# Two-layer decoder trunk on one core: first weight chunk plain, ScalarE's order unforced, one convolution tap on ScalarE, output projection all in high and low parts

## The chip, the cores and the metric

The kernel runs on one core of one Trainium2 chip. A core has a matrix engine (TensorE, PE), a vector engine (VectorE, DVE), a scalar engine (ScalarE, ACT), a general engine (GpSimd, POOL) and a queue engine (SyncE, SP) that issues the transfers from main memory. Each engine works through its own list of instructions in order and waits on semaphores for the others. The metric is the device time of one execution in microseconds; lower is better.

## What is computed

One sequence of 256 tokens with 1024 features goes through two layers. Each layer is a half-step SwiGLU feed-forward block, a token mixer, and another half-step feed-forward block. The mixer of layer 0 is stick-breaking attention, that of layer 1 a recurrent block (RG-LRU). Each block's input is normed and then scaled and shifted by numbers that come from a conditioning vector through a large matrix (`mod_w`), and its output is gated likewise. Everything is float32.

```python
for layer in range(DEPTH):
    mod = (c_act @ mod_w[layer] + mod_b[layer]).reshape(B, N_SUB, 3, D_MODEL)
    h, g = sublayer_input(x, norm_g[layer, 0], mod[:, 0])
    x = x + MACARON_W * g * swiglu(h, ffn_w_gu[layer, 0], ffn_w_down[layer, 0])
    h, g = sublayer_input(x, norm_g[layer, 1], mod[:, 1])
    y = mixer(h)
    x = x + g * y
    h, g = sublayer_input(x, norm_g[layer, 2], mod[:, 2])
    x = x + MACARON_W * g * swiglu(h, ffn_w_gu[layer, 1], ffn_w_down[layer, 1])
return rmsnorm(x, final_norm_g)
```

The recurrent block, cut to what the change touches (`xp` is `xb` with three zeros ahead of the first token, so that `conv_w[3]` is the tap on a token's own value):

```python
gate, xb = jnp.split(h @ w_in, 2, axis=-1)
xc = conv_b + xp[:, 0:S] * conv_w[0]
for tap in range(1, CONV_W):
    xc = xc + xp[:, tap:tap + S] * conv_w[tap]
r, i = sigmoid(blockwise xc @ w_r + b_r), sigmoid(blockwise xc @ w_i + b_i)
a = exp(-LRU_C * r * softplus(-lam)); b = sqrt(1 - a * a) * (i * xc)
hs = scan(a, b)
y = (gelu(gate) * hs) @ w_out
```

## The kernel before

Features lie on the 128 partitions and tokens along the free side, so x is eight tiles of 128 x 256. A weight block of 128 x 2048 (1 MB) is fetched by one transfer into one of three `raw` buffers.

**High and low parts.** Most products are made from parts. `load` (L510) converts each 1024-column half of a raw block into a high part `wh` on ACT (L525, a copy into a shorter format) and a low part `wl = raw - wh` on DVE (L528). Seven buffers of each kind stand in a ring. Activations are split alike, hi on ACT and lo on DVE. `Acc.group` (L541) then issues three matmuls for each product: wh with hi, wh with lo, wl with hi. `group32` (L565) instead issues one plain float32 matmul from unsplit data; the trace shows two instructions for it.

**The planner.** The program is not written in the order in which it runs. `Program.op` records each operation with an engine, a modelled cost, what it reads and writes and, with `after`, operations that it must follow. `schedule` (L170) then runs a model of the engines and emits the operations in the order of their modelled starts. An operation of ACT or DVE gets its due time from the PE work that needs it. So a change of one operation or of one ring can move others.

**Start.** `first_loads` (L1240) fetches the conditioning vector and x. Four small matmuls on zeros (`warm(EARLY)`), then two products that spread the vector over the partitions (L1247), then the sum of squares for the norm (`rstd`, L624 to L630) and eighteen more small matmuls (`warm(LATE)`, L842) run on PE. `norm_chunk` (L651) makes the first normed chunk: hp on DVE (L656), hi on ACT, lo on DVE (L658). The first feed-forward block starts by going through its first eight output tiles (SQ = 8) one input chunk k at a time, as the chunks arrive (L837 to L865): 16 groups for each k, into eight accumulators. The 1 MB of weights for chunk k come interleaved with the two 0.5 MB tiles of `mod_w` that chunk k + 1 needs. `early` (L800) reduces such a tile on DVE (L585) and makes a scale or a shift on ACT (`mf`). `first_chunk` (L822) makes hi and hp from them on ACT (seen as `hx<-arenaf,mf,mf` and `hpre<-arenaf,mf,mf`) and lo on DVE (L832). Chunks 0 and 7 (`SMALL`) come in four pieces of 512 columns, the others in two halves. For k = 1, 2, 3 (`FREE`) and the `SMALL` ones the order of ACT is left to the planner; for k = 4, 5, 6 both ACT operations of `first_chunk` must follow the conversion of the chunk's second half (`splits[:1]`, L858). After the first group of chunks 1, 3, 5, 7 `kick_op` (L740) issues one tiny matmul, which marks the chunk's beginning in the trace.

**Mod tiles.** The other 128 tiles of `mod_w` (0.5 MB each) are fetched all along the first two thirds of the kernel into a ring `rawm` of four buffers, and each is reduced by one DVE operation (L585) and one short one that reads its accumulator. They share SP's queue and DVE with the weights. The ring also holds the gate weights of the recurrent block (three loads) and, at the start, the conditioning vector.

**Recurrent block.** `rglru` (L1081) projects xb in five tiles; `conv` (L1089) has ACT write xb into one of two buffers and DVE make the four taps (L1095 for the first with the bias, L1098 for the others). `gates` (L1102) makes two plain products and three ACT functions for each of ten blocks, and a product on DVE (L1127) that frees one of the three buffers in which i stands. `decay`, `scan` and `output` (L1165 to L1197) are ordered by ACT's function tables: all exponentials, then all square roots, then all Gelu. Meanwhile PE makes four gate projections. `output(0)` ends with the DVE product L1189, which gives y0, the first of five blocks of 256 features. With `N32 = 1` block 0 and its weights stay unsplit, and `down` (L672) takes them with `group32`; the blocks after it are split (L1194, L1195) and go through `group`. `down` runs the first three blocks one after the other and the last two by pairs of output tiles, and then adds the result to x (L695).

Of the kernel before, what the change touches and what calls it, by code (L numbers as in the profile page):

```python
# [34 lines left out]
SMALL = (0, 7)  # L35
EARLY, LATE = 4, 18
KICK0, FREE = (1, 3, 5, 7), (1, 2, 3)
HXPAD, HKPAD, ARPAD = 112, 16, 56
# [331 lines left out]
def trunk(ctx, tc, xT, cb, par, modw, gu0, gu, wdn, qk, wv, wo, win, wri, wout, out):  # L370
# [22 lines left out]
    rawr, _ = ring("raw", 3, CH)  # L393
    modr, _ = ring("rawm", 4, D)
    whr, _ = ring("wh", 7, HALF, F32R)
# [111 lines left out]

    splits = []

    def load(src, n, name, chain=None, size=HALF):  # L510

        raw = Buf(rawr, name=f"raw_{name}")
        part = None
        if chain is None:
            dma(lambda: raw()[:, :n], src, n, [raw])
        res = []
        for a in range(0, n, size):
            m = min(n - a, size)
            if chain is not None:
                part = a  # L520
                chain(lambda a=a, m=m: raw()[:, a : a + m], src[:, a : a + m], m, [(raw, a)])
            h, lo = Buf(whr, name=f"wh_{name}"), Buf(wlr, name=f"wl_{name}")

            def fh(h=h, a=a, m=m):
                act.activation(h()[:, :m], raw()[:, a : a + m], AF.Copy)  # L525

            def fl(h=h, lo=lo, a=a, m=m):
                dve.tensor_tensor(lo()[:, :m], raw()[:, a : a + m], f32(h()[:, :m]), ALU.subtract)  # L528

            splits[:] = [pr.op("ACT", c_act(m), fh, [(raw, part)], [h]), V(fl, m, [(raw, part), h], [lo])]  # L530
            res.append((h, lo))
        return res
# [117 lines left out]

    def norm_chunk(gen, d, q):  # L651
        gs, sh = mfin[gen + (1,)], mfin[gen + (0,)]
        hp, hi, lo = Buf(hpr), Buf(hxr), Buf(hxr)
        hcur.setdefault(gen, []).append((hi, lo))
        c = slice(d, d + 1)
        V(lambda: dve.scalar_tensor_tensor(hp(), x[d](), gs()[:, c], q(), ALU.mult, ALU.mult), T, [x[d], (gs, d), q], [hp], ptr=1)  # L656
        A(lambda: hi()[:, :T], hp, AF.Identity, T, [hp, (sh, d)], [hi], ptr=1, bias=lambda: sh()[:, c])
        V(lambda: dve.scalar_tensor_tensor(lo()[:, :T], hp(), sh()[:, c], f32(hi()[:, :T]), ALU.add, ALU.subtract), T,  # L658
          [hp, (sh, d), hi], [lo], ptr=1)

    def norm(gen, q):
# [118 lines left out]
    def ffn(l, s, nxt, hook):  # L780
# [11 lines left out]
        if j == 0:  # L792
# [7 lines left out]
            def early(k, w):  # L800
# [20 lines left out]

            def first_chunk(k, after=()):  # L822

# [8 lines left out]
                pr.op("DVE", c_dve(T), lambda: dve.tensor_tensor(lo()[:, :T], hp(), f32(hi()[:, :T]), ALU.subtract), [hp, hi],  # L832
                      [lo])

            early(0, 1)
            early(0, 0)
            for k in range(KD):  # L837
                if k == 4:
                    chained(lambda: pars()[:, NP0:], par[:, NP0:], NPAR - NP0, [(pars, 1)])
                if k == 0:  # L840
                    norm_chunk((0, 0), k, q)
                    warm(LATE, [pr.last_pe])  # L842
                    for ks in xq_parts:
                        normed(ks)
                elif k in SMALL:
                    first_chunk(k)
# [234 lines left out]
    def rglru(l, s, nxt):  # L1081
        N32 = 1
        R, F = new_phase(8 * (NB - N32), 86)
# [5 lines left out]
        def conv(n, evict):  # L1089
            xb = Buf(xbr)  # L1090
            evict(n % 2, xb)
            if n % 2 == 0:
                xc[n // 2] = Buf(F, 4)
            c, e, cs = of(xc, n)
            V(lambda: dve.tensor_scalar(c()[:, cs], xb()[:, 1 : 1 + T], col(OFF_CW + n), col(OFF_CB + n), ALU.mult,  # L1095
                                        ALU.add), T, [xb, pars], [(c, e)], ptr=2)
            for tap in range(1, 4):
                V(lambda tap=tap: dve.scalar_tensor_tensor(c()[:, cs], xb()[:, 1 + tap : 1 + tap + T],  # L1098
# [141 lines left out]
    def first_loads(F):  # L1240
# [4 lines left out]
        for h in range(2):  # L1245
            cs = slice(h * 512, (h + 1) * 512)
            pr.op("PE", 1870.0, lambda h=h, cs=cs: pe.matmul(b[h]()[:, :], ones[:1, :], c()[:1, cs], start=True, stop=True),  # L1247
                  [c], [b[h]])
# [117 lines left out]
```

## Time and profile before

| | us |
|---|---|
| median of 3 runs | 962.55 |
| lowest and highest of the runs | 962.23, 963.67 |
| the profiled execution, its own time | 962.91 |
| its span, first to last instruction | 961.2 |

The profile is of one execution, taken by the hardware profiler. A group's row gives the line and engine, the operation, the tile written and the tiles read, the shape and the count, then after the bar the busy time and the mean duration in ns, and after a second bar the idle time of the engine just before those instructions with what ended it. A row of the timeline gives start, length, engine, line, operation, tiles and count, and in brackets the idle time before it with its releaser; a row with a count over one covers neighbouring instructions of one kind. A row of waits gives who waited for whom, the sum in us, the count and the longest. Matmuls overlap in the pipeline, so their number in a stretch says more of PE's pace than their durations.

### The profile page before, as it was taken

The page shows a single profiled execution, that of the slowest core. Times are in us where ns is not written, and L with a number is a line of the kernel's source. Part 1 is how long each engine was busy: PE and PEld are TensorE (multiplying, and loading weights), DVE is VectorE, ACT ScalarE, POOL GpSimd, SP SyncE. Part 2 cuts the span into 40 slices and gives each one's busy share as a digit, 9 for nine tenths or more (in the row PEclk, how much of TensorE's full clock was granted, in tenths as well). Part 3 has the DMA queues.
Part 4 walks back from the last instruction along what each step waited for, and adds up shares of the span by engine and source line. Part 5 has one row for each costly group of instructions (what it writes and reads, how often), then busy time and mean ns, then how long its engine had stood idle before and what let it go on. Part 6 is the DMA issues. An engine that isn't in the chain of part 4 may idle for free.

```text
span 961.2 us, 19726 instructions
## 1 busy us (share of the span) xinstructions
PE 949.2 (99%) x8132; PEld 936.2 (97%) x8132; DVE 791.8 (82%) x1291; ACT 570.1 (59%) x928; POOL 2.4 (0%) x15
## 2 busy tenths in 40 slices
PE   8999999999999999999999999999999999999996
PEld 6999999999999999999999999999999999999996
DVE  7899989798999999999799998855997996555443
ACT  6685544378886854454466545534879785445333
POOL 1000000000000000000000000000000000000000
PEclk9999999999999999999999999999999999999998
DMA  9979999945666489999976998965243746545531
GB/s 345 405 293 376 355 347 366 363 158 193 244 215 225 174 320 359 357 349 352 350 282 243 342 344 317 351 244 209 88 166 143 264 160 238 208 184 193 172 119 44
DMA packets 48044, 251.25 MB, mean 261 GB/s; under 512 B 5457, under 2 KB 6097, under 8 KB 28242
## 3 DMA queue, kind: packets, MB, share of 16 engines
q1 hardware_dynamic: 47378, 249.43, 69.8%
q8 instruction: 63, 1.03, 0.4%
q10 hardware_dynamic: 576, 0.56, 0.2%
q14 instruction: 27, 0.22, 0.1%
HBM read 248.92 MB, written 1.05 MB: 260 GB/s over the span
## 4 chain that ended last, share of the span: by engine, by line
PE 80%; DVE 8%; DMA 7%; ACT 3%; issue 2%; SPq 0%; DVEq 0%; ACTq 0%
PE bank L553 73%; DMA rawm<-in_modw 5%; DVE wl L528 2%; PE bank L919 2%; DVE arenaf L1098 1%; DMA raw<-in_gu 1%; PE bank L1042 1%; ACT arenaf L502 1%; PE bank L570 1%; ACT wh L525 1%; DVE rawm L585 1%; PE bank L630 1%; PE bank L995 1%; PE bank L1020 1%; DVE arenar L585 0%
## 5 line engine op out<-in xcount | busy, mean ns | idle before, releaser
L553 PE MATMUL bank<-hx,wh 128*128 128x256 f32 (+1 forms) x3236 | 560.5, 278 | 1.8 <-DVE hx L832 1.3
L525 ACT ACTIVATE wh<-raw 128x1024 fp32r<-128x1024 f32 (+1 forms) x328 | 336.2, 1046 | 282.1 <-PE bank L553 204.3
L553 PEld LDWEIGHTS bank<-hx,wh 128*128 128x128 f32 x3236 | 490.1, 188 | 3.8 <-DVE hx L832 1.8
L528 DVE TENSOR_TENSOR wl<-raw,wh 128x1024 fp32r<-128x1024 f32 (+1 forms) x328 | 389.2, 1208 | 105.4 <-ACT wh L525 104.9
L553 PE MATMUL bank<-hx,wl 128*128 128x256 f32 (+1 forms) x1618 | 448.0, 277 | 0.1
L553 PEld LDWEIGHTS bank<-hx,wl 128*128 128x128 f32 x1618 | 304.3, 188 | 0.3 <-DVE wl L528 0.3
L553 PE MATMUL bank<-arenar,wh 128*128 128x256 f32 x1664 | 285.0, 277 | 0.0
L553 PEld LDWEIGHTS bank<-arenar,wh 128*128 128x128 f32 x1664 | 250.6, 188 | 0.1
L553 PE MATMUL bank<-arenar,wl 128*128 128x256 f32 x832 | 229.7, 276 | 0.0
L585 DVE SCALAR_TENSOR_TENSOR rawm<-rawm,cact 128x1024 f32<-128x1024 f32 x128 | 155.6, 1220 | 20.8 <-DMA rawm<-in_modw 20.0
L553 PEld LDWEIGHTS bank<-arenar,wl 128*128 128x128 f32 x832 | 156.2, 188 | 0.0
L502 ACT ACTIVATE arenar<-a 128x256 fp32r<-128x256 f32 x88 | 35.4, 406 | 11.4 <-DVE a L773 10.8
L778 DVE TENSOR_TENSOR arenar<-a,arenar 128x256 fp32r<-128x256 f32 x88 | 36.4, 419 | 1.0 <-ACT arenar L502 1.0
L502 ACT ACTIVATE sg<-bank 128x256 f32<-128x256 f32 x82 | 29.8, 368 | 9.7 <-PE bank L553 9.7
L773 DVE TENSOR_TENSOR a<-bank,sg 128x256 f32<-128x256 f32 x82 | 34.1, 418 | 0.5 <-ACT sg L502 0.3
L553 PE MATMUL bank<-hk,wh 128*128 128x256 f32 x156 | 31.2, 291 | 0.0
L502 ACT ACTIVATE hx<-x,mf 128x256 fp32r<-128x256 f32 x40 | 18.5, 500 | 19.5 <-DVE x L695 19.5
L695 DVE SCALAR_TENSOR_TENSOR x<-bank,mf,x 128x256 f32<-128x256 f32 x48 | 21.6, 478 | 7.8 <-PE bank L553 7.7
L553 PEld LDWEIGHTS bank<-hk,wh 128*128 128x128 f32 x156 | 24.0, 188 | 0.5
L502 ACT ACTIVATE hx<-hpre,mf 128x256 fp32r<-128x256 f32 x41 | 19.9, 499 | 6.2 <-DVE hpre L656 5.4
L919 PE MATMUL bank<-wh,hx 128*128 128x256 f32 x128 | 23.4, 280 | 0.0
L502 ACT ACTIVATE arenaf<-arenaf 128x768 f32<-128x768 f32 (+1 forms) x31 | 22.0, 737 | 0.4
(115 smaller groups left out, 573.4 us busy)
## 6 DMA issues: line engine op xcount, KB each, us to landing
raw<-in_gu SPq DMA_DIRECT2D x79, 1024.0 KB, 6.0
rawm<-in_modw SPq DMA_DIRECT2D x128, 512.0 KB, 7.5
raw<-in_wdn SPq DMA_DIRECT2D x44, 1024.0 KB, 5.9
raw<-in_win SPq DMA_DIRECT2D x10, 1024.0 KB, 4.7
arenar<-in_modw SPq DMA_DIRECT2D x16, 512.0 KB, 9.7
raw<-in_qk SPq DMA_DIRECT2D x8, 1024.0 KB, 4.9
raw<-in_gu SPq DMA_DIRECT2D x14, 512.0 KB, 9.2
raw<-in_wout SPq DMA_DIRECT2D x5, 1024.0 KB, 5.2
```

The costliest lines, as they stand in the source:

```text
L502: act.activation(o(), i(), f, **{k: (v() if callable(v) else v) for k, v in kw.items()})
L525: act.activation(h()[:, :m], raw()[:, a : a + m], AF.Copy)
L528: dve.tensor_tensor(lo()[:, :m], raw()[:, a : a + m], f32(h()[:, :m]), ALU.subtract)
L553: pe.matmul(o(b()), wc(u()), xc(v()), start=start and n == 0, stop=stop and n == len(passes) - 1, skip_group_check=True)
L570: pr.op("PE", c_mm(n, 4), lambda: pe.matmul(o(b()), wc(w()), xc(x32()), start=start, stop=stop, skip_group_check=True), [w, x32] + ([] if ...
L585: dve.scalar_tensor_tensor(raw(), raw(), 1.0, cact(), ALU.mult, ALU.mult, accum_out=m()[:, t : t + 1])
L630: pr.op("PE", c_mm(T, 4), lambda i=i, q=q, c=c: pe.matmul(b()[:, :T], ones, q()[:, c], start=i == 0, stop=i == len(qs) - 1), [q] + [b] * ( ...
L695: dve.scalar_tensor_tensor(x[d](), acc.b()[:, j * T : (j + 1) * T], gate()[:, d : d + 1], x[d](), ALU.mult, ALU.add)
L773: V(lambda: dve.tensor_tensor(a(), b()[:, T:], sg(), ALU.mult), T, [(b, (1, 0)), sg], [a])
L778: V(lambda: dve.tensor_tensor(y[1](), a(), f32(y[0]()), ALU.subtract), n, [a, y[0]], [y[1]])
L919: pe.matmul(o, u()[:, tb * P : (tb + 1) * P], v()[:, c0 : c0 + 256], start=start and n == 0, stop=k == KD - 1 and n == 2, skip_group_check ...
L995: pe.matmul(zb[e]()[:, BL[i]], v()[rows, kc], w()[rows, qc], start=False, stop=i == 1 and n == 2, skip_group_check=True)
```

## The change

- `MID = 4`: `first_loads` issues four more small matmuls on zeros on PE, behind the two products L1247.
- `PLAIN = 4`: the four weight pieces of chunk 0 of the first projections are not split. `norm_chunk` makes one more copy of that chunk, unsplit (`h0`, on ACT, ahead of hi), and `plain_group` makes each of the chunk's 16 products as one plain float32 matmul from `raw` and `h0`. Four ACT conversions and four DVE subtractions go.
- `first_chunk` no longer has an `after`, and is recorded ahead of the chunk's load for every k.
- `conv`: ACT makes the tap on a token's own value with the bias from xb; DVE adds the other three.
- `N32 = 0`: block 0 of the output projection is split like the others, its weights and y0 too; the tiny matmul moves to block 0 (`kicks=(N32,)`).
- The ring `rawm` has three buffers instead of four; the arena of the recurrent block is larger by the same 4 KB per partition.

```diff
-EARLY, LATE = 4, 18
-KICK0, FREE = (1, 3, 5, 7), (1, 2, 3)
+EARLY, MID, LATE = 4, 4, 18
+KICK0, PLAIN = (1, 3, 5, 7), 4
...
-    modr, _ = ring("rawm", 4, D)
+    modr, _ = ring("rawm", 3, D)
...
-    def load(src, n, name, chain=None, size=HALF):
+    def load(src, n, name, chain=None, size=HALF, plain=0):
...
+            if len(res) < plain:
+                res.append((raw, part))
+                continue
...
-            splits[:] = [pr.op("ACT", c_act(m), fh, [(raw, part)], [h]), V(fl, m, [(raw, part), h], [lo])]
+            pr.op("ACT", c_act(m), fh, [(raw, part)], [h])
+            V(fl, m, [(raw, part), h], [lo])
...
-    def norm_chunk(gen, d, q):
+    def norm_chunk(gen, d, q, whole=False):
...
+        h = None
+        if whole:
+            h = Buf(hpr)
+            A(h, hp, AF.Identity, T, [hp, (sh, d)], [h], ptr=1, bias=lambda: sh()[:, c])
...
+        return h
...
+            def plain_group(acc, g, raw, part, c0):
+
+                b, start = acc.b, g == 0
+                acc.started = True
+                pr.op("PE", c_mm(T, 4), lambda: pe.matmul(b()[:, g * T : (g + 1) * T], raw()[:, c0 : c0 + P], h0(),
+                                                          start=start, stop=False, skip_group_check=True),
+                      [(raw, part), h0] + ([] if start else [(b, "start")]),
+                      [(b, (g, 0))] + ([(b, "start")] if start else []))
...
-            def first_chunk(k, after=()):
+            def first_chunk(k):
...
-                    A(o, xk, AF.Identity, T, [(xq, part), (gs, k), (sh, k)], [hp if o is hp else hi], ptr=2, after=after[:1],
+                    A(o, xk, AF.Identity, T, [(xq, part), (gs, k), (sh, k)], [hp if o is hp else hi], ptr=2,
...
-                    norm_chunk((0, 0), k, q)
+                    h0 = norm_chunk((0, 0), k, q, PLAIN > 0)
...
-                elif k in SMALL:
+                else:
                     first_chunk(k)
...
-                ws = load(gu0[k], CH, f"gu0_{k}", chain, size)
-                if k not in SMALL:
-                    first_chunk(k, splits[:1] if k not in FREE else ())
+                plain = PLAIN if k == 0 else 0
+                ws = load(gu0[k], CH, f"gu0_{k}", chain, size, plain)
...
+                        if i < plain:
+                            plain_group(accs[f], g, *ws[i], (f * 2 + g) * P)
+                            continue
...
-        N32 = 1
+        N32 = 0
...
-            V(lambda: dve.tensor_scalar(c()[:, cs], xb()[:, 1 : 1 + T], col(OFF_CW + n), col(OFF_CB + n), ALU.mult,
-                                        ALU.add), T, [xb, pars], [(c, e)], ptr=2)
-            for tap in range(1, 4):
+
+            A(lambda: c()[:, cs], lambda: xb()[:, 4:], AF.Identity, T, [xb, pars], [(c, e)], ptr=2,
+              scale=lambda: col(OFF_CW + 3 * NR + n), bias=lambda: col(OFF_CB + n))
+            for tap in range(3):
...
+        warm(MID, [pr.last_pe])
```

More of the change, by code (lines that the diff above doesn't have):

```diff
@@ L506, in V @@
         return pr.op("DVE", cost or c_dve(n) + 62.0 * ptr, fn, r, w)
-    splits = []
-    def load(src, n, name, chain=None, size=HALF):
+    def load(src, n, name, chain=None, size=HALF, plain=0):
         raw = Buf(rawr, name=f"raw_{name}")
@@ L829, in first_chunk @@
                 for o in (lambda: hi()[:, :T], hp):
-                    A(o, xk, AF.Identity, T, [(xq, part), (gs, k), (sh, k)], [hp if o is hp else hi], ptr=2, after=after[:1],
+                    A(o, xk, AF.Identity, T, [(xq, part), (gs, k), (sh, k)], [hp if o is hp else hi], ptr=2,
                       scale=lambda: gs()[:, k : k + 1], bias=lambda: sh()[:, k : k + 1])
-                pr.op("DVE", c_dve(T), lambda: dve.tensor_tensor(lo()[:, :T], hp(), f32(hi()[:, :T]), ALU.subtract), [hp, hi],
-                      [lo])
+                V(lambda: dve.tensor_tensor(lo()[:, :T], hp(), f32(hi()[:, :T]), ALU.subtract), T, [hp, hi], [lo])
             early(0, 1)
```

## The prediction

> **What bounds the kernel now.** I read the page of the profile first, then the busy time of the engines in stretches, then the order of the instructions at the start and around the output projection.
>
> ```profile
> span 961.2 us, 19726 instructions
> ...
> PE 949.2 (99%) x8132; PEld 936.2 (97%) x8132; DVE 791.8 (82%) x1291; ACT 570.1 (59%) x928; POOL 2.4 (0%) x15
> ```
>
> TensorE (PE) is busy for 949.2 of 961.2 us. The next view tells whether that is one unbroken stretch.
>
> ```profile
> 30.00:35.00 5.00, 4.77 (x42) 4.53 (x41) 4.64 (x8) 3.48 (x6) 0.00 (x0) 1.00 1.03 411
> 35.00:40.00 5.00, 4.43 (x37) 4.07 (x36) 4.54 (x6) 3.18 (x5) 0.00 (x0) 1.00 1.02 403
> 40.00:45.00 5.00, 4.54 (x40) 4.30 (x39) 3.82 (x7) 3.59 (x6) 0.00 (x0) 1.00 1.03 411
> ...
> 45.00:742.00 697.00, 696.83 (x6033) 691.61 (x6031) 616.39 (x1027) 425.08 (x699) 0.00 (x0) 1.00 0.76 282
> ```
>
> The columns are the stretch, its length, then busy time and count of PE, weight loads, VectorE (DVE), ScalarE (ACT) and GpSimd, the granted clock, the DMA share and GB/s. From 45 to 742 us PE lacks 0.17 us. Between 30 and 45 us it lacks 1.26 us, with the DMA engines full. So there are three places where the change can act: the first 45 us, the output projection of the recurrent block behind 742, and any new hole in the unbroken stretch, where one microsecond gained or lost reaches the end whole. Two paces are needed below.
>
> ```profile
> 320.68 97.45 PE bank L553 x855
> ...
> 742.23 7.17 PE L570 MATMUL bank<-arenaf,raw 128*128 128x256 f32 x32 [0.33 <-DVE arenaf L1189]
> ```
>
> A high/low matmul takes 97.45/855 = 0.114 us, so a group of three 0.342 us. The plain form (L570) makes two instructions of each matmul: 7.17 us less the 0.38 us that the last one runs, over 31 steps, is 0.219 us, so a group 0.438 us. Sixteen groups are 5.47 us in parts and 7.0 us plain.
>
> **Start: first chunk plain, order unforced, MID.** The rows of the start, in order of time:
>
> ```profile
> 2.53 3.75 PE L1247 MATMUL bank<-rawm,ones 1*128 1x512 f32 x4 [0.33 <-POOL a L469]
> 7.32 3.54 PE L630 MATMUL bank<-arenaf,ones 128*128 128x256 f32 x8 [1.05 <-DVE arenaf L1269]
> 7.97 0.69 DVE L1269 TENSOR_TENSOR arenaf<-arenaf 128x512 f32<-128x512 f32 x1
> 10.70 2.13 PE L1237 MATMUL bank<-zero 128*128 128x256 bf16 x18
> 10.87 0.08 DVE L585 DVE_READ_ACCUMULATOR arenar<-arenar,cact 128x1 f32 x1
> 10.96 0.47 ACT L502 ACTIVATE rms<-bank,eps 128x256 f32<-128x256 f32 x1 [0.73 <-PE bank L630]
> 11.92 0.48 DVE L656 SCALAR_TENSOR_TENSOR hpre<-x,mf,rst 128x256 f32<-128x256 f32 x1 [0.96 <-ACT rst L502]
> 12.62 0.51 ACT L502 ACTIVATE hx<-hpre,mf 128x256 fp32r<-128x256 f32 x1
> 13.18 0.38 PE L553 MATMUL bank<-hx,wh 128*128 128x256 f32 x1 [0.35 <-ACT hx L502]
> ...
> 16.59 0.33 SPq L495 DMA_DIRECT2D raw<-in_gu  x1
> ...
> 20.08 0.20 PE L740 MATMUL bank<-ident,zero 128*128 128x64 bf16 x1
> ```
>
> The first product waits for the normed chunk (12.62 + 0.51), not for the weights, so the plain copy h0, which takes the place of hx there, starts it at 13.18 again. Chunk 0 then costs 7.0 us: end at 20.2. Before, its 5.47 us of work, with holes for the splits, ended just ahead of 20.08, the first group of chunk 1 (the marker L740 follows that group). So the plain form loses about half a microsecond here, and frees ACT of four conversions and DVE of four subtractions; h0 adds one ACT copy (0.51) that nothing waits behind, since hi and lo of chunk 0 are wanted only by later tiles.
>
> What decides is where this stage is held up last:
>
> ```profile
> 40.18 1.22 DVE L585 SCALAR_TENSOR_TENSOR arenar<-arenar,cact 128x1024 f32<-128x1024 f32 x1
> 41.04 1.06 ACT L525 ACTIVATE wh<-raw 128x1024 fp32r<-128x1024 f32 x1 [1.96 <-DMA raw<-in_gu]
> ...
> 42.60 0.60 ACT L502 ACTIVATE hx<-arenaf,mf,mf 128x256 fp32r<-128x256 f32 x1
> ...
> 43.73 0.42 DVE L832 TENSOR_TENSOR hx<-hpre,hx 128x256 fp32r<-128x256 f32 x1 [1.18 <-ACT hpre L502]
> ...
> 44.21 0.39 PE L553 MATMUL bank<-hx,wh 128*128 128x256 f32 x1 [0.46 <-DVE hx L832]
> ```
>
> This is chunk 5, one of 4, 5, 6 whose modulation (hx, hpre) is forced behind the conversion of the chunk's second weight half. ACT sat idle 1.96 us for that half at 41.04; only then came hx, and PE waited to 44.21. Behind it PE never waits again in this stage. Without the force the modulation needs only the reduction of its mod tile, 40.18 + 1.22 = 41.4 (which itself stood behind work that DVE no longer has), 0.3 us for the last of the two short scale/shift operations, and the 1.6 us from hx (42.60) to the end of lo (44.15). The edit therefore takes this hold from about 44.1 to 43.3 or earlier. PE would arrive at chunk 5 at 20.2 + 4 x 5.47 + 0.15 for two markers = 42.2. So PE gains 44.1 - 42.2 = 1.9 us at most if nothing holds it, and 0.8 us if the hold stays at 43.3. The extra 1.5 us of plain products is inside this number. The raw buffer of chunk 0 is now read until 20.2; the transfers of chunk 3 into it stand in SP's queue behind that, and all later ones behind them. I cost that at nothing because about eight transfers of 0.5 MB, 10 us of work for the DMA engines at 400 GB/s, are under way; without that cover it would be up to 3.6 us (20.2 less an issue at 16.6).
>
> MID puts four small matmuls on PE in the 1.05 us hole ahead of L630. The eight L630 instructions run at (3.54 - 0.39)/7 = 0.45 us, twice the 0.219 us of L570: a PE at half pace although the granted clock column says 1.00. At full pace the last four, free at 7.97 + 0.69, would end near 9.7 and not at 10.86. But hpre also needs DVE, free at 10.95, so it can move from 11.92 to 10.95: between 0 and 0.95 us. I take 0.4, and 0.4 off again for holds that remain: start 1.9 us.
>
> The Trainium skill (TensorE: Matmul & The Clock Gate, Part 1) says that the clock goes from half to full after one busy window of about 3.4 us, and that the window is free-running, so the turn varies by run. The trace agrees in kind: half pace from 7.32, and from 10.70 on the eighteen small matmuls of L1237 go at (2.13 - 0.28)/17 = 0.109 us, full pace. By that rule MID would pay in some runs and not in others; a run in which it pays fully is the first rival.
>
> **Convolution tap on ACT.**
>
> ```profile
> L1095 DVE TENSOR_SCALAR arenaf<-xb,pars 128x256 f32<-128x256 f32 x10 | 4.1, 409 | 0.0
> L502 ACT ACTIVATE xb<-tr,bc 128x256 f32<-128x256 f32 x4 | 1.9, 499 | 0.0
> 690.00:725.00 35.00, 35.00 (x273) 33.95 (x272) 34.37 (x71) 27.02 (x54) 0.00 (x0) 1.00 0.44 160
> ```
>
> DVE, full in this stage (34.37 of 35), loses ten operations of 0.41 us; ACT gets ten like the xb copy, 0.50 to 0.60 us (5 to 6 us), into 7.98 us of idle time. PE is unbroken there, so by itself this is worth nothing; it moves when the first output block y0 is ready, which is the next term.
>
> **Output projection in parts.** Chunk 0 of it goes from 7.0 to 5.47 us on PE: 1.55 us saved. But y0 and its weights must now be split.
>
> ```profile
> 739.73 0.63 ACT L502 ACTIVATE arenaf<-arenaf 128x512 f32<-128x512 f32 x1
> 741.50 0.67 DVE L1189 TENSOR_TENSOR arenaf<-arenaf 128x512 f32<-128x512 f32 x1
> 742.22 1.04 ACT L525 ACTIVATE wh<-raw 128x1024 fp32r<-128x1024 f32 x1
> ...
> L502 ACT ACTIVATE arenar<-arenaf 128x512 fp32r<-128x512 f32 x4 | 2.5, 628 | 1.9 <-DVE arenaf L1189 1.9
> L1195 DVE TENSOR_TENSOR arenar<-arenaf,arenar 128x512 fp32r<-128x512 f32 x4 | 2.7, 685 | 0.0
> 725.00:742.00 17.00, 16.90 (x149) 16.70 (x147) 11.31 (x17) 16.93 (x30) 0.00 (x0) 1.00 0.29 106
> ```
>
> Gelu (739.73) and the product (741.50) gave y0 at 742.17; PE had been waiting 0.33 us. The split adds 0.63 on ACT and 0.69 on DVE, 1.3 us in a row, all on PE's path. Two weight halves add 2.1 us on ACT and 2.4 on DVE. DVE has 5.7 us free in 725 to 742, ACT has none. Best case: freed DVE brings the gates' products forward by 2 us or more and the conversions fall in ACT's gaps ahead of 725; then neither wait remains: gain 1.55 + 0.33 = 1.9. Worst: all added ACT work (5.0 + 2.1 + 0.6 = 7.7 us) with half of the idle 7.98 usable, 3.7 us late plus the split. I take the split alone as exposed, with the rest covered: 1.55 + 0.33 - 0.33 - 1.3 = 0.25, and 0.35 of DVE's relief that must arrive: gain 0.6.
>
> **Three buffers for mod tiles instead of four.**
>
> ```profile
> DVE rawm L585 <- DMA rawm<-in_modw: 20.0, 21, 3.8
> ACT wh L525 <- PE bank L553: 204.3, 113, 3.5
> 320.00:380.00 60.00, 17.17 (x28) 1.00 0.84 314
> ```
>
> DVE waited 20.0 us for mod tiles in 21 of 128 cases and PE saw none of it: ACT's commonest wait is for PE to free a converted weight buffer (204.3 us), so seven halves, 7 x 2.73 = 19 us of PE work, mostly lie ready. I cost the lost buffer at 0; below nothing it can't go, as PE has nothing to win there; above, the last rival.
>
> **Sum.** The profiled execution took 962.91 us (span 961.2 and 1.7 around it), 0.36 above the median of 962.55. 962.9 - 1.9 - 0.6 = 960.4 from it, 960.05 from the median: I say 960.2.
>
> **Rivals.** *MID pays fully and no hold remains*: start 1.9 + 0.95, tail 0.6, so 959.3. For it: PE's half pace ahead of 10.5. Against it, in the same rows: L1247 kept PE busy from 2.53 to 6.28 and the pace was still halved.
>
> *ACT becomes the bound in the recurrent block*: y0 comes 1 to 3.7 us later than at 742.17, plus 1.3 for its split, less 1.55. That takes 0.75 to 3.4 of the 1.9 us won at the start: 961.4 to 964.1, middle 962.5, no difference that can be told. For it: ACT's 16.93 of 17.00 us ahead of 742. Against: most of ACT's idle time in 690 to 725 was waiting for the DVE that is relieved.
>
> *Slower: mod tiles starve DVE behind the attention block.* In 320 to 380 us 14 tiles are reduced (28 instructions, two a tile). If each waited 20.0/21 = 0.95 us, that is 13.3 us of delay for the weight splits queued behind them on DVE. In this window DVE also has its fullest load:
>
> ```profile
> 340.00:360.00 20.00, 20.00 (x179) 20.00 (x178) 19.82 (x31) 11.20 (x18) 0.00 (x0) 1.00 0.84 307
> ```
>
> With 0.2 us free in 20, some 12.7 us stays. The ready halves of 2.73 us cover it if five lie there, but here they are only being filled: with three PE loses 4.5 us and the kernel is at 964.5, with two 7.2 us and 967. It decides from 4.4 us lost; middle 965.7. Against it: the order is planned anew for three buffers, and the stage reduced more tiles than its due list asks for.
>
> *The change doesn't do what it says at the start*: the planner, unforced, may choose the old order, and the hold at 44.2 stays: 962.1. It counts with the second rival.
>
> **How the numbers follow.** Forecast 0.38; MID in full 0.17; ACT bound or old order 0.20; starved DVE 0.25. A measurement tells 0.2% (1.9 us) from no change: faster is below 960.6. Of the forecast 0.33 is faster and 0.05 same (it is 0.4 us from that bound), of the ACT rival 0.18 same and 0.02 slower. Faster 0.50, same 0.23, slower 0.27. The range: best start (2.85) with best tail (1.9) is 957.8 from the median; above it takes in the ACT rival and half of the slower one, 965.5. The forecast's own range is 958.8 to 961.6.
>
> **What would show it.** Right: two-instruction matmuls of chunk 0 start near 13 or before and end near 20; no PE wait over 0.3 us between 30 and 45; chunk 5 at 42 to 43; PE's wait ahead of the first output group under 1.7 us; 45 to the output projection unbroken. Wrong: a PE wait on wl in 60 to 680 us, L585 waiting for mod tiles far above 20 us in sum, or PE idle over 2 us ahead of the output projection with ACT full.

## The result and the profile after

| | before | after |
|---|---|---|
| median, 22 runs each (us) | 962.44 | 963.98 |
| lowest and highest | 961.82, 964.02 | 961.01, 966.92 |
| the profiled execution, its own time | 962.91 | 963.24 |
| its span | 961.2 | 961.5 |

The ratio is 1.0014, with a 95% interval of 1.0009 to 1.002: 1.5 us slower, where 960.2 us, faster than before, was forecast. The size lies inside the 0.2% that counts as no change, but the sign is the other one.

First the page of the kernel after: span and busy time.

```profile
span 961.5 us, 19790 instructions
...
PE 949.7 (99%) x8136; PEld 937.5 (98%) x8136; DVE 790.1 (82%) x1280; ACT 575.0 (60%) x938; POOL 2.4 (0%) x15
```

PE is busy for nearly the same time (949.7 us, before 949.2), so the question is again where it stands still. A fixed mark in both programs is the first matmul of each sum-of-squares product (`ssq`), one for every norm. Those at both ends of the recurrent block, with PE's two waits in it, in the timeline of the kernel after:

```profile
681.47 0.59 PE L632 MATMUL bank<-ssq,ones 128*128 128x256 f32 x2
...
741.40 0.38 PE L555 MATMUL bank<-arenar,wh 128*128 128x256 f32 x1 [1.02 <-ACT arenar L502]
...
742.52 0.39 PE L555 MATMUL bank<-arenar,wh 128*128 128x256 f32 x1 [0.74 <-DVE arenar L1213]
...
777.28 0.59 PE L632 MATMUL bank<-ssq,ones 128*128 128x256 f32 x2
```

and the same marks before:

```profile
683.00 0.59 PE L630 MATMUL bank<-ssq,ones 128*128 128x256 f32 x2
...
776.95 0.59 PE L630 MATMUL bank<-ssq,ones 128*128 128x256 f32 x2
```

Up to the recurrent block the change has won 683.00 - 681.47 = 1.53 us. The block itself lasts 95.81 us where it lasted 93.95, a loss of 1.86. The difference, 0.33, is that of the spans (961.5 - 961.2). Not all of the 1.53 is the change's: 1.04 of it is there at the first norm mark (201.86 after, 202.90 before), the attention stage behind that lasts 0.30 longer after, and 0.79 comes from the next two stages, which last 181.55 and 181.37 us in this execution of the kernel before and 181.06 or 181.07 in most of the other profiles.

**The start.** PE's timeline of the kernel after (L632 was L630, L747 was L740, L824 is `plain_group`):

```profile
12.52 7.17 PE L824 MATMUL bank<-hpre,raw 128*128 128x256 f32 x32 [0.23 <-ACT hpre L502]
19.89 0.20 PE L747 MATMUL bank<-ident,zero 128*128 128x64 bf16 x1
31.20 0.38 PE L555 MATMUL bank<-hx,wh 128*128 128x256 f32 x1 [0.46 <-ACT hx L502]
32.15 0.38 PE L555 MATMUL bank<-hx,wh 128*128 128x256 f32 x1 [0.57 <-DVE hx L848]
```

Chunk 0 runs in two-instruction matmuls from 12.52 to 19.69, and the holds at 38 and 44 us are gone. One remains, at chunk 3, in two parts. The busy time of 30 to 45 us hides what a hold costs, because the matmul behind a hold counts as busy for its whole 0.38 us, while in the unbroken flow one starts every 0.11 us; the count of matmuls does not:

```profile
30.00:45.00 15.00, 13.97 (x120) 13.50 (x119) 14.02 (x23) 10.73 (x18) 0.00 (x0) 1.00 1.03 407
```

and before:

```profile
30.00:45.00 15.00, 13.74 (x114) 12.90 (x113) 13.01 (x19) 10.24 (x16) 0.00 (x0) 1.00 1.03 408
```

Without a hold this stretch has 135 matmuls (run 12 below), 0.111 us each. So 15 of them are missing after and 21 before: 1.7 and 2.3 us, where the idle times say 1.03 and 1.26. What holds up chunk 3 shows on ACT of the kernel after:

```profile
25.57 1.06 ACT L526 ACTIVATE wh<-raw 128x1024 fp32r<-128x1024 f32 x1 [1.33 <-DMA raw<-in_gu]
...
30.21 0.29 ACT L502 ACTIVATE mf<-mr,pars 128x1 f32<-128x1 f32 x1 [0.75 <-DVE arenar L587]
```

A weight half came late by transfer, and the scale operation that releases the chunk's modulation then waited for DVE to reduce its mod tile. In run 1 below, which has no hold, the same conversion begins at 24.23 and the same scale operation at 29.08, both over 1.1 us earlier. PE also comes sooner here: its marker of chunk 1 is at 19.89, that of run 1 at 20.61.

**The output projection.** ACT's timeline in the kernel after, from the squares to the high part of y0:

```profile
728.33 2.70 ACT L502 ACTIVATE arenaf<-arenaf 128x512 f32<-128x512 f32 x5
730.93 1.99 ACT L526 ACTIVATE wh<-raw 128x1024 fp32r<-128x1024 f32 x2
732.94 1.28 ACT L1329 ACT_TABLE_LOAD   x1
...
738.25 0.63 ACT L502 ACTIVATE arenaf<-arenaf 128x512 f32<-128x512 f32 x1
...
740.72 0.63 ACT L502 ACTIVATE arenar<-arenaf 128x512 fp32r<-128x512 f32 x1 [0.86 <-DVE arenaf L1207]
```

and before, where the table load follows at once:

```profile
731.71 2.70 ACT L502 ACTIVATE arenaf<-arenaf 128x512 f32<-128x512 f32 x5
```

Read both from the norm matmul at the head of the stage. The squares begin at 46.86 us of it after (728.33 - 681.47) and at 48.71 before: the stage in front of them is 1.85 us faster. But between the squares and the load of the function table for the roots now stand the two weight halves of output block 0, 1.99 us, and the first Gelu begins at 56.78, where it began at 56.73 (739.73). What had been gained is spent in full. Behind Gelu, on DVE of the kernel after:

```profile
740.02 0.67 DVE L1207 TENSOR_TENSOR arenaf<-arenaf 128x512 f32<-128x512 f32 x1
740.60 0.68 DVE L1200 TENSOR_TENSOR_SCAN arenaf<-arenaf 128x256 f32<-128x256 f32 x1
741.20 0.67 DVE L1197 TENSOR_TENSOR arenaf<-arenaf 128x512 f32<-128x512 f32 x1
741.78 0.68 DVE L1213 TENSOR_TENSOR arenar<-arenaf,arenar 128x512 fp32r<-128x512 f32 x1
```

y0's product (L1207) ends at 740.69, its low part (L1213) at 742.46, 1.77 us later, because two operations of later blocks stand between. PE, which came at 741.40 - 1.02 = 740.38, waits first for the high part and then for the low one: 1.76 us where it waited 0.33. Then the granted clock falls, as PE's windows of one microsecond show (the clock is the third figure from the end: 0.65, 0.50, 0.50, 0.64):

```profile
743.00:744.00 1.00, 1.00 (x8) 1.00 (x7) 1.00 (x3) 1.00 (x2) 0.00 (x0) 0.65 0.00 0
744.00:745.00 1.00, 1.00 (x6) 1.00 (x6) 1.00 (x2) 1.00 (x3) 0.00 (x0) 0.50 0.00 0
745.00:746.00 1.00, 1.00 (x7) 1.00 (x6) 1.00 (x2) 1.00 (x2) 0.00 (x0) 0.50 0.00 0
746.00:747.00 1.00, 1.00 (x8) 1.00 (x8) 1.00 (x2) 1.00 (x2) 0.00 (x0) 0.64 0.24 33
```

That is 4 - 2.29 = 1.71 us of PE work lost. Together: 1.43 more waiting, plus 1.71, less the 1.55 that the form in parts saves by the pace of the matmuls, is 1.6 of the 1.86 us.

### The profile page after: what moved, and what is told of

Its sections match the earlier page's. It is cut to its first block, busy times and chain, and to the rows that moved or that the text cites. A ratio compares the mean times of both kernels' runs of the same rounds, so it can differ in the third digit from the quotient of the medians.

```text
span 961.5 us, 19790 instructions
## 1 busy us (share of the span) xinstructions
PE 949.7 (99%) x8136; PEld 937.5 (98%) x8136; DVE 790.1 (82%) x1280; ACT 575.0 (60%) x938; POOL 2.4 (0%) x15
## 3 DMA queue, kind: packets, MB, share of 16 engines
q8 instruction: 63, 1.03, 0.4%
## 4 chain that ended last, share of the span: by engine, by line
PE 92%; DMA 3%; ACT 2%; DVE 2%; issue 0%; DVEq 0%; SPq 0%
PE bank L555 86%; PE bank L936 2%; DMA raw<-in_gu 2%; ACT arenaf L502 1%; PE bank L1059 1%; PE bank L1012 1%; PE bank L1037 1%; PE bank L1134 1%; DVE wl L529 0%; DMA x<-in_xT 0%; ACT wh L526 0%; DVE arenaf L1200 0%; PE bank L632 0%; PE bank L1039 0%; ACT L1329 0%
## 5 line engine op out<-in xcount | busy, mean ns | idle before, releaser
L555 PE MATMUL bank<-hx,wh 128*128 128x256 f32 (+1 forms) x3204 | 553.9, 278 | 1.0 <-DVE hx L848 0.6
L555 PEld LDWEIGHTS bank<-hx,wh 128*128 128x128 f32 x3204 | 485.0, 188 | 1.9 <-DVE hx L848 0.8
L529 DVE TENSOR_TENSOR wl<-raw,wh 128x1024 fp32r<-128x1024 f32 (+1 forms) x326 | 389.5, 1215 | 113.1 <-ACT wh L526 112.1
L555 PE MATMUL bank<-hx,wl 128*128 128x256 f32 (+1 forms) x1602 | 443.5, 277 | 0.0
L555 PE MATMUL bank<-arenar,wh 128*128 128x256 f32 x1696 | 292.2, 278 | 1.8 <-ACT arenar L502 1.0
L555 PEld LDWEIGHTS bank<-arenar,wh 128*128 128x128 f32 x1696 | 256.9, 189 | 2.2 <-ACT arenar L502 1.2
L555 PE MATMUL bank<-arenar,wl 128*128 128x256 f32 x848 | 234.9, 277 | 0.0
L587 DVE SCALAR_TENSOR_TENSOR rawm<-rawm,cact 128x1024 f32<-128x1024 f32 x128 | 155.6, 1221 | 14.7 <-DMA rawm<-in_modw 13.9
L555 PEld LDWEIGHTS bank<-arenar,wl 128*128 128x128 f32 x848 | 159.9, 189 | 0.0
```

The lines of the kernel that those rows point to most:

```text
L555: pe.matmul(o(b()), wc(u()), xc(v()), start=start and n == 0, stop=stop and n == len(passes) - 1, skip_group_check=True)
L587: dve.scalar_tensor_tensor(raw(), raw(), 1.0, cact(), ALU.mult, ALU.mult, accum_out=m()[:, t : t + 1])
```

## Experiments

The reading to test, called A in the expectations: the start wins about what was forecast, the third mod buffer and the tap on ACT cost nothing, and the output projection in parts takes back more than the start won. The other letters are rivals and are told where they stand. Each run is compared with the kernel before on the same chip.

**1. Output chunk plain again, all else as after.**

```diff
-        N32 = 0
+        N32 = 1
```

> The changed kernel with only the output projection undone (block 0 unsplit again, three mod buffers kept). Theory A (the tail eats the start's gain: PE waits for the split of y0 and then runs at half pace for some 3 us): PE's wait ahead of the projection returns to about 0.3 us, no half pace, time 961.0 us, 1.4 under the kernel before and 3 under the changed one. Theory B (three mod buffers or the convolution's ACT work cost it): stays within 0.7 us of 964.

Measured 960.98 (959.92 to 963.24), ratio 0.9985 (0.9976 to 0.9994): faster than before. Its timeline, with the marks, y0's product and the plain output groups (L572):

```profile
680.60 0.59 PE L632 MATMUL bank<-ssq,ones 128*128 128x256 f32 x2
...
737.88 0.67 DVE L1207 TENSOR_TENSOR arenaf<-arenaf 128x512 f32<-128x512 f32 x1
...
739.35 6.85 PE L572 MATMUL bank<-arenaf,raw 128*128 128x256 f32 x31
...
773.96 0.59 PE L632 MATMUL bank<-ssq,ones 128*128 128x256 f32 x2
```

The stage lasts 93.36 us, 2.45 less than after. y0 is ready at 57.95 of it, 1.27 earlier than after (59.22), and PE does not wait at all. The edit that was to save 0.6 us costs 3.0 by the medians. The stage is also 0.59 shorter than before, with the convolution's tap on ACT and y0 in good time.

**2. Before, with the output chunk in parts and three mod buffers.**

```diff
-    modr, _ = ring("rawm", 4, D)
+    modr, _ = ring("rawm", 3, D)
...
-        N32 = 1
+        N32 = 0
```

> The kernel before with the output projection all in parts and three mod buffers, nothing else. Theory A: PE waits 1.5 to 2.5 us ahead of the projection, part of the runs then show half pace; 963.5 to 965 us. Theory B by the convolution alone: 962.5, since the convolution is still on DVE.

Measured 967.01 (966.04 to 968.36), ratio 1.0047 (1.0035 to 1.006): worse than expected. PE's longest wait in this run:

```profile
PE bank L553 <- ACT arenar L502: 2.9, 1, 2.9
```

and the row of ACT's timeline between the squares and the table load, which begins at 735.81:

```profile
733.80 2.00 ACT L525 ACTIVATE wh<-raw 128x1024 fp32r<-128x1024 f32 x2
```

The two weight halves stand at the same place, and without the tap on ACT there is no relief to pay for them: 4.7 us over the 962.34 of before. Behind the waits the granted clock is at half again, from about 744.0 to 750.8 us, twice as long as after.

**3. Only the convolution's tap on ACT.**

```diff
-            V(lambda: dve.tensor_scalar(c()[:, cs], xb()[:, 1 : 1 + T], col(OFF_CW + n), col(OFF_CB + n), ALU.mult,
-                                        ALU.add), T, [xb, pars], [(c, e)], ptr=2)
-            for tap in range(1, 4):
+            A(lambda: c()[:, cs], lambda: xb()[:, 4:], AF.Identity, T, [xb, pars], [(c, e)], ptr=2,
+              scale=lambda: col(OFF_CW + 3 * NR + n), bias=lambda: col(OFF_CB + n))
+            for tap in range(3):
```

> The kernel before with only the convolution's own-token tap on ACT. Theory A: 962.4 +- 0.4, PE is unbroken there either way. Theory D (5 us more on ACT delay the chain to y0): PE's wait ahead of the projection grows from 0.33 to 1 to 2 us, 963.5.

Measured 962.18, ratio 1.0001 (0.9992 to 1.001). By itself it is worth nothing, as forecast. Its profile is not quite that simple: PE's wait for y0 is gone, but the order made anew has waits of 0.36 us at 775.32, where the stage ends, and of 0.57 at 783.82, so the stage lasts 93.98 us.

**4. The kernel after with that tap back on DVE** (the diff of run 3 reversed).

> The kernel after (964.0) with the convolution's own-token tap on VectorE again. If that tap on ScalarE is what pays for the split output chunk (before_split_proj lost 4.6 us where the whole change has this loss without it): 965.0 to 967.0. If the ten operations on ScalarE make ScalarE the bound ahead of Gelu: 962.5 to 963.5. If neither: 964.0 within 0.4.

Measured 965.97 (965.22 to 967.89), ratio 1.0042 (1.0029 to 1.0055), 2 us over after: with the output chunk in parts the tap on ACT pays. PE's waits of this run, 3.61 us against 1.76:

```profile
742.92 0.38 PE L555 MATMUL bank<-arenar,wh 128*128 128x256 f32 x1 [2.87 <-ACT arenar L502]
744.05 0.58 PE L555 MATMUL bank<-arenar,wh 128*128 128x256 f32 x1 [0.74 <-DVE arenar L1212]
```

The granted clock behind them is still at half in the window of 749 to 750 us:

```profile
749.00:750.00 1.00, 1.00 (x7) 1.00 (x6) 1.00 (x2) 1.00 (x3) 0.00 (x0) 0.50 0.58 221
```

**5. Is it the clock?** Ten matmuls on zeros ahead of the output projection keep PE at work during its wait.

```diff
+        pr.op("PE", WARM_OUT * 109.0, busy, [], [fill], [pr.last_pe])
```

> The changed kernel with ten small matmuls on zeros (1.1 us) on PE between the last gate projection and the output projection. Theory A with the clock as half of the loss: the half pace behind the wait goes, 962.3 us, about 1.7 under the changed kernel, and the runs lie closer together. Theory C (only the wait for the split counts, the half pace is of this one profile): 964.0, no change.

Measured 963.70 (962.53 to 965.82), ratio 1.0013 (1.0004 to 1.0021): nearer to C than to A's 962.3. But the profile has no half pace, and the stage shortens by 0.91 to 94.90 us, though PE still waits for y0's two parts behind the zeros:

```profile
682.41 0.59 PE L633 MATMUL bank<-ssq,ones 128*128 128x256 f32 x2
...
744.17 0.38 PE L556 MATMUL bank<-arenar,wh 128*128 128x256 f32 x1 [0.86 <-DVE arenar L1214]
...
777.31 0.59 PE L633 MATMUL bank<-ssq,ones 128*128 128x256 f32 x2
```

PE gets y0's low part at 61.76 us of this stage (744.17 - 682.41), and at 61.05 in that of after (742.52 - 681.47). It starts 0.71 us later and ends 0.91 us earlier, so the half pace costs about 1.6 us in the profiled execution of after, close to the 1.71 read from its clock. The time shows little of it because of those 0.71 us and because the order made anew for this program has two waits in the attention block that after has not (0.38 and 0.41 us, at 202.04 and 210.55); that stage lasts 118.24 us here and 117.48 after.

**6 and 7. Can the parts be had in a better order?** In 6 the two weight conversions on ACT are forced behind the first Gelu, out of the chain of table loads:

```diff
-    def load(src, n, name, chain=None, size=HALF, plain=0):
+    def load(src, n, name, chain=None, size=HALF, plain=0, after=()):
...
-            pr.op("ACT", c_act(m), fh, [(raw, part)], [h])
+            pr.op("ACT", c_act(m), fh, [(raw, part)], [h], after)
...
-                ws += load(srcs[c], CH, f"dn_{l}_{s}_{c}")
+                ws += load(srcs[c], CH, f"dn_{l}_{s}_{c}", after=behind if c == 0 else ())
```

In 7, besides, the roots are recorded apart from the scans, and the scans of the blocks from the third on stand behind y0's product.

> The kernel after (964.0) with ScalarE's conversion of the two weight halves of the first output block forced behind the first Gelu, so that it leaves the chain squares, table load, roots, table load, Gelu. Theory A (the conversions inside this chain delay the split of y0 by their 2.0 us and cause PE's wait): y0's high part about 1.5 to 2 us earlier, PE's wait ahead of the output projection below 1.2 us, time 962.0 to 963.0; the weights must not become the later of the two. Theory C (DVE with its scans ahead of y0's product is what ends last): y0 at most 0.5 us earlier, 963.5 to 964.2.

> As after_weights_late, and the scans of the third and later blocks on VectorE stand behind the product of y0. Theory A and C together: PE's wait ahead of the output projection below 0.8 us and no half pace behind it, time 960.0 to 961.5. If the wait stays at 1.8 us: 964.0.

Measured 963.04 (ratio 1.001, 0.9999 to 1.0021) and 963.79 (1.0015, 1.0006 to 1.0024). Run 6 lies just above what A expected, and its interval takes in no change; run 7 misses. Both have new waits in the attention block, as run 5 has, and that stage lasts 118.23 and 118.22 us in them, 0.75 more than after, so their times say less than the stage of the output projection does. DVE's and PE's timeline of run 6, whose stage begins at 682.44:

```profile
739.67 0.66 DVE L1207 TENSOR_TENSOR arenaf<-arenaf 128x512 f32<-128x512 f32 x1
...
740.86 2.35 DVE L529 TENSOR_TENSOR wl<-raw,wh 128x1024 fp32r<-128x1024 f32 x2
743.13 0.68 DVE L1213 TENSOR_TENSOR arenar<-arenaf,arenar 128x512 fp32r<-128x512 f32 x1
...
743.86 0.38 PE L555 MATMUL bank<-arenar,wh 128*128 128x256 f32 x1 [2.40 <-DVE arenar L1213]
```

y0's product comes 1.3 us earlier in the stage than after (57.23 against 58.55), so the place of the conversions was indeed what delayed it. But the weights' low parts (L529), which now come later, take DVE for 2.35 us between the product and y0's low part, and PE waits 2.40 us. In run 7, whose stage begins at 683.54, the weights' low parts stand ahead of y0's low part too, but it begins at 59.02 us of the stage (60.69 in run 6), and PE's wait for y0 falls to 0.74 us, as was expected. A second wait came in its place, for the low part of a later block, whose scan had been put behind y0's product:

```profile
743.30 0.39 PE L555 MATMUL bank<-arenar,wh 128*128 128x256 f32 x1 [0.74 <-DVE arenar L1217]
...
762.44 0.39 PE L555 MATMUL bank<-arenar,wh 128*128 128x256 f32 x1 [1.72 <-DVE arenar L1217]
```

The stage lasts 94.55 and 94.90 us in these two, with the clock at full pace in both profiled executions. With run 5 that makes three orders without the half pace, and all of them are 0.6 to 1.0 us above the 93.95 of before. Whether the parts can win is not settled: run 7's stage less its second wait would be 93.18 us, an estimate, and an order without that wait, or one in which DVE makes y0's low part ahead of the weights' low parts, was not tried.

**8 to 11. The start, taken apart.** On top of run 1: chunk 0 in parts again (`PLAIN = 0`); the modulations of chunks 4 to 6 forced behind the conversion again, and those of chunks 1 to 6 recorded behind the load; no MID; four mod buffers.

```diff
-KICK0, PLAIN = (1, 3, 5, 7), 4
+KICK0, PLAIN = (1, 3, 5, 7), 0
```

> The kernel after with the plain output chunk of before (as in after_plain_proj, 960.98) and with chunk 0 of the first projections in high and low parts again; the unforced order, MID, the convolution tap on ScalarE and three mod buffers stay. Theory A (the start's gain needs both: the plain chunk frees four conversions and four subtractions of the engines that supply PE, the unforced order moves the modulations ahead): the holds at the chunks 3 to 5 come back in part, first norm matmul at 201.5 to 202.3, time 961.3 to 962.2. Theory B (the unforced order does it all, the plain chunk's 1.5 us of extra products are a loss): 959.5 to 960.6.

```diff
-            def first_chunk(k):
+            def first_chunk(k, after=()):
...
+                if k and k not in SMALL:
+                    first_chunk(k, splits[:1] if k not in (1, 2, 3) else ())
```

> The kernel after with the plain output chunk (960.98 in after_plain_proj) and with the modulations of the chunks 4, 5 and 6 forced behind the weight conversion again, as in before. Theory A: the holds return, first norm matmul at 202.0 to 202.9, time 961.7 to 962.4. Theory B (the order does it all): the same, 962.0 to 962.6. If the order was worth nothing: 961.0.

```diff
-        warm(MID, [pr.last_pe])
```

> The kernel after with the plain output chunk (960.98 in after_plain_proj) and without the four MID matmuls. If MID is worth what the forecast took for it: 961.4. If it does not decide the pace of the eight first matmuls: 961.0 within 0.3.

```diff
-    modr, _ = ring("rawm", 3, D)
+    modr, _ = ring("rawm", 4, D)
```

> The kernel after with the plain output chunk (960.98 in after_plain_proj) and with four buffers for the mod tiles instead of three. If three buffers cost nothing, as PE's unbroken stretch of 60 to 680 us says: 961.0 within 0.4. If the third buffer's late transfers hold the start or VectorE: 960.2 or less.

| run | us | ratio to before |
|---|---|---|
| 1 (their base) | 960.98 | 0.9985 (0.9976 to 0.9994) |
| 8, chunk 0 in parts | 963.81 | 1.0011 (1.0003 to 1.002) |
| 9, order forced | 961.83 | 0.9993 (0.9984 to 1.0001) |
| 10, no MID | 961.40 | 0.9986 (0.9978 to 0.9995) |
| 11, four mod buffers | 960.35 | 0.9975 (0.9965 to 0.9985) |

Run 8 lies above all that was expected. PE's timeline of it, with the markers of chunks 1 and 7:

```profile
20.56 0.20 PE L747 MATMUL bank<-ident,zero 128*128 128x64 bf16 x1
...
38.05 0.38 PE L555 MATMUL bank<-hx,wh 128*128 128x256 f32 x1 [0.34 <-DVE hx L848]
...
44.01 0.39 PE L555 MATMUL bank<-hx,wh 128*128 128x256 f32 x1 [0.23 <-DVE hx L848]
...
55.95 0.20 PE L747 MATMUL bank<-ident,zero 128*128 128x64 bf16 x1
```

and the same markers in its base, run 1:

```profile
20.61 0.20 PE L747 MATMUL bank<-ident,zero 128*128 128x64 bf16 x1
...
53.67 0.20 PE L747 MATMUL bank<-ident,zero 128*128 128x64 bf16 x1
```

The three holds of before are back although the order is free (the first, 0.24 us, at 31.85), so the free order alone does not remove them: the plain chunk, which takes conversions and subtractions off ACT and DVE, is needed too. A new wait of 1.19 us at 204 us, in front of the attention block, is made by the order planned anew and is not the start's; with it the 2.8 us of the time can't be read as the plain chunk's worth. The markers can: from chunk 1 to chunk 7 run 1 takes 33.06 us, run 8 35.39, before 35.49, after 34.64 and run 9 34.31. So in these executions the plain chunk is worth 2.3 us and the free order 1.25, each given the other; against that, the plain form costs 0.38 us more from chunk 0's first product to the marker of chunk 1 (7.27 in run 1, 6.89 in run 8). By its time run 9 is 0.85 us above its base, the direction of A, with overlapping intervals. MID (0.4 us) and the fourth buffer (0.6) can't be told from nothing, though run 10 stands where MID's forecast worth would put it; run 11 lies between its two expectations. For three buffers the waits of the kernel after speak more plainly, 13.9 us in 18 cases where before had 20.0 in 21, with PE busy for all of the 680.00 us from 60 to 740:

```profile
DVE rawm L587 <- DMA rawm<-in_modw: 13.9, 18, 2.4
```

**12. The start alone.** Run 11 with the convolution's tap on DVE, so that only the plain first chunk, the free order and MID differ from before.

> Only what the change does at the start (plain first chunk, unforced order, MID): the output chunk is plain, the convolution's tap is on VectorE and the mod tiles have four buffers, all three as before. If the start is worth what the forecast took (1.9 us) and the rest nothing: 960.4 to 960.9 beside a before of 962.4, and the stage from the norm matmul at 683 to the one at 777 lasts 93.9 to 94.3 as in before. If the convolution's tap gives more than PE's 0.33 us wait ahead of the output projection (93.36 for this stage with it in after_plain_proj): the time is 961.0 or more. If the start is worth only what the first norm matmul of the kernel after showed (1.04 us): 961.2 to 961.6.

Measured 961.06 (960.48 to 963.06) beside a before of 962.85, ratio 0.9985 (0.9975 to 0.9994): 1.8 us by the medians, 1.4 by the ratio, whose interval runs from 0.6 to 2.4. That does not tell the 1.9 us of the forecast from the 1.04 of after. The timeline speaks more plainly. From the first product of chunk 0 to the marker of chunk 7 PE takes 40.42 us here (13.53 to 53.95) and 42.39 before (13.18 to 55.57), 1.97 less. When that first product comes is another matter: it varies from 12.52 to 14.68 over the profiles, whatever the edit. The stretch of 30 to 45 us:

```profile
30.00:45.00 15.00, 15.00 (x135) 14.93 (x133) 14.08 (x23) 10.67 (x17) 0.00 (x0) 1.00 1.02 406
```

and in PE's timeline the marks of the stage and the output groups:

```profile
680.61 0.59 PE L632 MATMUL bank<-ssq,ones 128*128 128x256 f32 x2
...
739.82 6.53 PE L572 MATMUL bank<-arenaf,raw 128*128 128x256 f32 x29 [0.31 <-DVE arenaf L1206]
...
774.54 0.59 PE L632 MATMUL bank<-ssq,ones 128*128 128x256 f32 x2
```

No hold is left, and the stage lasts 93.93 us, that of before to 0.02, with PE's old wait of 0.31 in it. Run 11, which has the lowest median here and is the version to keep, differs from this one by the tap alone, and PE does not wait there. The two can't be told apart by their times, but the stage can: it lasts 93.36 us in runs 1 and 8 to 11, all with the tap on ACT and the output chunk plain, 0.57 less than here.

## Why the prediction was wrong

**The start was right.** 1.9 us were forecast, the start alone gives 1.4 to 1.8, and 1.97 from the first product to chunk 7 in its profile. The way was right in the main: chunk 0 ends near 20, the holds at 38 and 44 us go. The forecast put this down to the free order above all; by run 8 the holds stay without the plain chunk. The longer use of chunk 0's raw buffer, put at nothing, cost nothing: PE is unbroken from 30 to 45 us in run 12. In the kernel after itself the start gives less (1.04 us at the first norm matmul), because a hold of 1.03 us stays at chunk 3, behind a late transfer. Runs 1 and 12, with the same start, don't have it; whether it is in all executions of the kernel after is open. The forecast's 0.4 us off for remaining holds named such a thing and was too small for this execution.

**MID** was taken at 0.4; without it the time is 0.4 higher, within the error. The eight first products last 3.04 us in the kernel after and up to 3.78 in other runs with MID, where they lasted 3.54 before, so it does not set their pace reliably.

**Three buffers** and **the tap alone** cost nothing that the times tell, as forecast. The attention stage lasts 117.18 us before and in runs 11 and 12, all with four buffers, and 117.40 to 117.48 in after and in runs 1, 2, 4 and 8 to 10, with three; run 3, with four, has 117.34, so some 0.1 to 0.3 us may go there. The slower rival (DVE starved behind the attention block) is false: PE is unbroken there.

**The failed step is the sum of the output projection**, as it stood: "I take the split alone as exposed, with the rest covered: 1.55 + 0.33 - 0.33 - 1.3 = 0.25, and 0.35 of DVE's relief that must arrive: gain 0.6." Each term against the trace:

- The saving on PE, 1.55, is borne out roughly: run 6's stage less its wait of 2.40 us is 92.15, 1.2 below run 1's 93.36, and that counts no slower matmuls behind the wait.
- "The rest covered" is wrong. The forecast looked for cover in "ACT's gaps ahead of 725". ACT did fill those gaps, as the row below shows beside 27.02 us before, but with the taps (run 1, with the taps and the plain chunk, has 32.87 there, run 12, without them, 27.52); the conversions came at 730.93, between two links of the one chain that leads to y0, and cost it 1.99 us. That used up the 1.85 us by which the stage had come earlier, of which the forecast had put down 0.35 as gain.
- The split of y0 took 1.77 us behind the product, not 1.3, as DVE did two operations of later blocks first. PE waited 1.76 us, where the forecast's terms leave about 1.3.
- The half pace behind the wait (1.71 us of PE work lost in this execution) was in no term. A wait was priced at its length. It is the largest part of the 2.46 us between the 0.6 forecast as gain and the 1.86 lost.

The row for the second of these, in the windows of the kernel after:

```profile
690.00:725.00 35.00, 35.00 (x273) 33.95 (x272) 32.44 (x60) 32.93 (x65) 0.00 (x0) 1.00 0.52 181
```

The rival *ACT becomes the bound in the recurrent block* (961.4 to 964.1, middle 962.5) holds the measured time at its upper end, but in part by luck. ACT's chain did eat what was gained, as it says; yet it has y0 1 to 3.7 us later, and y0's product ends at 59.22 us of the stage after and 59.17 before. Without the half pace, which is not in that rival either, the time would be about 963.98 - 1.6 = 962.4, an estimate, near its middle. It was given 0.20, together with the old order at the start, against 0.38, because "most of ACT's idle time in 690 to 725 was waiting for the DVE that is relieved". ACT did fill that time, but this is beside the point: the added work had to stay out of the chain from 728 to 741, and in 725 to 742 ACT was already busy 16.93 of 17.00 us, a row that stood in the prediction.

Runs 1, 2 and 4 show that it is the output projection in parts that costs the time, and that the tap on ACT only softens it. Runs 6 and 7 show that DVE is short there as well: with the conversions out of ACT's chain, PE waits for y0's low part or for that of a later block. Run 1's stage is 2.45 us shorter than that of after. Of that, 1.6 to 1.7 us is the half pace, by run 5 and by the clock's record; the waits of 1.76 less the saving of 1.55 give 0.2, and some 0.5 us has no place in these figures. The rest of the 3.0 us between the two is ahead of the stage, which begins 0.87 us earlier in run 1, mostly for the hold at chunk 3. All this is read from one execution of each kernel; the runs of after spread from 961.01 to 966.92, and how many of them had the half pace is not known.

## What to carry to other kernels

Saving time on the busiest engine by giving its helpers more to do pays where the helpers have slack at that place; look at the few microseconds ahead of the consumer, at what a conversion would stand between, and not at the stage's share. At the start the reverse paid: with a plain chunk that is dearer on PE by 1.5 us at the pace of its matmuls, but frees the helpers where they are the ones late, 1.4 to 1.8 us were won. And count matmuls in a stretch, not busy time, to see what a wait costs.

## What the hardware showed that was not expected

Two waits of 1.02 and 0.74 us, with one matmul between, were followed by half pace from about 743.3 to 746.7 us; the two of 2.87 and 0.74 in run 4 by half pace from about 743.2 to 750.0; the two of 2.89 and 0.55 in run 2 by the same length, 6.8 us; a single wait of 2.40 us in run 6 by none. The Trainium skill (TensorE: Matmul & The Clock Gate, Part 1) has the clock judged in free-running windows of about 3.4 us, with a fall after a window of idleness. The length of the slow stretch after, 3.4 us, agrees, those of runs 2 and 4 are twice that, and a fall that depends on where a wait lies in such a window would fit that 1.76 us brought one and 2.40 did not; no run here shows the windows themselves. That waits of 1.76 us in sum suffice is shorter than the page's window of idleness, and the measurement decides.
